# Feed-forward strips of 256 columns with a 512-column product over both halves of x, and two entry strips in turns, in a hybrid decoder trunk

## The chip, the core and the metric

The kernel runs on one core of one Trainium2 chip. The metric is the device time of one execution, in microseconds (us), median of the runs shown. The engines are named as in the profile: PE is TensorE's matmul, PEld its weight load, DVE is VectorE, ACT ScalarE, POOL GpSimd, SP the SyncE queue that issues the DMAs.

## The reference

Two decoder layers over 256 tokens of width 2048, in float32. The first has an S5 and an RWKV-7 mixer, the second a Hawk recurrent block; each layer ends with a dense SwiGLU feed-forward part of inner width 5632. Each of the four parts stands between two RMS norms with a residual. Only the feed-forward part and the norms ahead of it are touched:

```python
def swiglu(h, w_gate, w_up, w_down):
    return (jax.nn.silu(h @ w_gate) * (h @ w_up)) @ w_down

# in each layer, after the mixer:
h = rms_norm(x, norm_ffn_pre[layer])
x = x + rms_norm(swiglu(h, ffn_w_gate[layer], ffn_w_up[layer], ffn_w_down[layer]),
                 norm_ffn_post[layer])
```

## The kernel before

Activations stand transposed: features on the 128 partitions, in chunks k of 128, and the 256 tokens along the free axis. A matrix product takes a 128 x 128 block of the weight as stationary operand and a chunk of x (128 x 256) as moving operand. Float32 accuracy comes from three products in fp32r: weight and x are each split into a high and a low part, and hi by x-high, hi by x-low and lo by x-high are added up in PSUM (L513, L514, L515 in `Strip.run`). That is a block of three products, each with its own weight load.

Weights arrive in chunks of 512 KB: 128 partitions by 2 rows of k by 512 columns (`fetch`, SP's queue, the tile `raw`). `ready` splits a chunk: ACT copies it into `hi` (L136), DVE subtracts into `lo` (L112). From the middle of the program on the rings of raw, hi and lo are four deep, and `Strip.take` has a chunk's split issued some three chunks ahead of its use. A strip is 512 output columns over all of k: four output tiles in two PSUM banks (`psw`, two generations, so that the next strip uses the other pair).

A feed-forward part (`ffn`) goes in two halves of the inner width. A half has 11 strips of gate and up (256 columns of each), evacuated by `gate` (multiply by the norm's factor `rb`, Silu, multiply, split into `hhi` and `hlo`), then four strips of the down product over the half's 22 chunks of the hidden vector; the first half's sums are copied to `y` (`first_evac`), the second's are added (`last_evac`), with their squares summed for the next norm.

Between the parts stands `post`. It makes the norm's factor (`token_rstd`, `rstd_steps`), then, chunk by chunk, the residual sum `xr` (DVE and POOL), x-high `xh` (ACT) and x-low `xl` (DVE). The first strip behind it, the entry strip, runs while x is being made: before each of its eight chunk pairs `before(g)` issues the making of the next two x chunks, `behind(g)` their squares. The factor of the norm itself is only known at the end of the entry (`finish`), so the entry strip's evacuation waits for it (`late`, `lazy`). There are three entries: two into a feed-forward part, one into the Hawk block.

The order on each engine is the order in which the program issues. Small work (evacuations, norms) is put into lanes of generators and issued between the products when a planner's clock `L.now` says that its inputs are due; `L.now` goes up by a fixed amount per block.

Of the kernel before, what the change touches and what calls it, by code (L numbers as in the profile page):

```python
# [67 lines left out]
def build(tc, a, out):  # L68
# [149 lines left out]
    with ctx:  # L218
# [185 lines left out]
        def fetch(upto):  # L404
            while nraw[0] < min(upto, len(groups)):
                w, g = groups[nraw[0]]
                wp = ring(nraw[0], "raw")
                t = wp.tile([P, 2, w.shape[3]], F32, tag="raw", bufs=1 if wp is wps[1] else 3, name="raw")
                SY.dma_start(t, w[g])
                clk["D"] = max(clk["D"], splt.get(nraw[0] - RAW[0], 0.0)) + 1.46 * w.shape[3] / 512  # L410
# [4 lines left out]
        def ready(upto):  # L415
            while nhi[0] < min(upto, len(groups)):
# [4 lines left out]
                W = raw.shape[2]  # L421
                hi = wp.tile([P, 2, W], F32R, tag="hi", bufs=1 if wp is wps[1] else 3, name="hi")
                lo = wp.tile([P, 2, W], F32R, tag="lo", bufs=1 if wp is wps[1] else 3, name="lo")
# [36 lines left out]
        class Strip:  # L460
# [19 lines left out]
            def take(self, g, less=0):  # L480
# [65 lines left out]

        def strip(w, x, widths, evac, hook=None, tail=False, mid=None, lazy=False, lane="ev"):
# [6 lines left out]

        W4 = [P] * 4

        def of2(z):

            return lambda k: (z[0][k // 8][:, k % 8, :], z[1][k // 8][:, k % 8, :])

# [12 lines left out]
        w_fg = [[a["w_fg"][l, i] for i in range(22)] for l in range(2)]  # L573
        w_fd = [[[a["w_fd"][l, h, s] for s in range(4)] for h in range(2)] for l in range(2)]

        def plan_ffn(l):
            for h in range(2):
                plan(*w_fg[l][11 * h:11 * h + 11], *w_fd[l][h])
# [1001 lines left out]
        def post(y, ssq, gpost, gpre):  # L1580
# [4 lines left out]
            xs = ([slot8(name="xh0"), slot8(name="xh1")], [slot8(name="xl0"), slot8(name="xl1")])  # L1585
            sx = Ssq(1)
            keep_warm(7)
            got, at = {}, {}

            def add(k, e):  # L1590
                t, xk = tmp1(("pn", "cs", "sw", "av")[k % 4]), xr[:, k]
                stt(V, t, y[k // 8][:, k % 8], vc(gpost, k), rs, MUL, MUL)
                if k == 1:
                    low(0)
                tt(e, xk, xk, t, ADD)

            def high(k):
                act(xs[0][k // 8][:, k % 8], xr[:, k], AF.Copy, scale=vc(gpre, k))

            def low(k):  # L1600
                stt(V, xs[1][k // 8][:, k % 8], xr[:, k], vc(gpre, k),
                    xs[0][k // 8][:, k % 8].bitcast(F32), MUL, SUB)
                at[k] = clk["V"] + 0.13

            def before(g):
                if g == 0:
# [6 lines left out]
                for k in (2 * g + 2, 2 * g + 3):  # L1613
                    if k < 16:
                        high(k)
                for k in (2 * g + 2, 2 * g + 3):
                    if k < 16:
                        low(k)
                    if k < 14:
                        add(k + 2, G)  # L1620
                if g == 6:
                    rel(rs)

            def behind(g):
                sq = sx.place()
                act(sq, xr[:, 2 * g:2 * g + 2], AF.Square)
                sx.pair(sq)
                if g == 7:
# [13 lines left out]
            return of2(xs), (before, behind, at.get), got  # L1642

        def ffn(l, x, mid, rstd, fp, gain=None):
            y = None
            rb = []
            for hf in range(2):
                hh = [fp.tile([P, 22, T], F32R, tag=n, name=n) for n in ("hhi", "hlo")]
                have = set()

                def late(i):
# [5 lines left out]
                    return f  # L1657

                def gate(i):
                    def f(ps):  # L1660
# [7 lines left out]
                        def rest():  # L1668
# [3 lines left out]
                            split(hh[0][:, 2 * i:2 * i + 2], hh[1][:, 2 * i:2 * i + 2], ga)  # L1672
                            have.add(i)
# [11 lines left out]
                def need(g):  # L1685
                    if g not in have:
                        L.drain("ev")
                        assert g in have

                for s in range(4):  # L1690
                    strip(w_fd[l][hf][s], of1(hh), W4, last_evac(y, s, ssq, True, gain) if hf else first_evac(y, s),
                          need, tail=bool(hf and s == 3))
# [30 lines left out]
        with tc.tile_pool(name="f0", bufs=1) as fp:  # L1723
            y, ssq = ffn(0, x, mid, rstd, fp)
            x, mid, rstd = post(y, ssq, "n0d", "n1a")


        with tc.tile_pool(name="hk", bufs=1) as hk:
# [81 lines left out]
            for n in range(8):  # L1810
                strip(w_oi[n], x, W4, hawk(n), lane="hx", **({} if n else dict(mid=mid, lazy=True)))
# [46 lines left out]
def pack(inp):  # L1858
# [56 lines left out]
    fg, fd = [], []  # L1915
    for l in range(2):
        k = np.stack([kt(g[n][l]).reshape(8, 2, P, 22, 256) for n in ("ffn_w_gate", "ffn_w_up")], 4)
        fg.append(k.transpose(3, 0, 2, 1, 4, 5).reshape(22, 8, P, 2, 512))
        fd.append(np.stack([strips(g["ffn_w_down"][l][2816 * j:2816 * j + 2816], 512) for j in range(2)]))
    o["w_fg"] = f(np.stack(fg))  # L1920
    o["w_fd"] = f(np.stack(fd))
# [4 lines left out]
          "w_fd", "s5lam", "s5bc", "s5d", "w2a2", "g2"]  # L1926
# [17 lines left out]
```

## Time and profile before

| | us |
|---|---|
| median of 3 runs (2434.27 to 2438.75) | 2435.07 |
| the profiled execution | 2434.1 |
| its span, first to last instruction | 2432.3 |
| PE busy | 2358.0 (97%) |
| DVE busy | 1457.4 (60%) |
| ACT busy | 1180.8 (49%) |

Busy time counts an instruction from its start to its modelled end, so products that overlap in the pipeline make PE look full; the distance from one product's start to the next says more. Times in the views are us from the span's start unless marked ns. The granted clock is a share of TensorE's full 2.4 GHz.

### The profile page before, as it was taken

What the parts mean: (1) busy time and instruction counts of PE and PEld (TensorE: products, weight loads), DVE (VectorE), ACT (ScalarE), POOL (GpSimd) and SP (SyncE); (2) the same over time, 40 slices, a digit from 0 to 9 for tenths busy, and PEclk for the clock granted to TensorE, in tenths of its full rate; (3) what the DMA queues carried; (4) which work ended last, traced back from release to release, by engine and by line L of the source; (5) the groups of instructions that cost most, each with busy time, mean ns of one, the idle gap of its engine ahead of it and who ended that gap; (6) DMA issues with size and microseconds to landing.
All of it is one profiled execution on the core that took longest, in us unless ns stands there. A gap on an engine that the chain in (4) does not pass through costs nothing.

```text
span 2432.3 us, 47365 instructions
## 1 busy us (share of the span) xinstructions
PE 2358.0 (97%) x19830; PEld 2313.1 (95%) x19830; DVE 1457.4 (60%) x2002; ACT 1180.8 (49%) x1550; POOL 410.5 (17%) x589
## 2 busy tenths in 40 slices
PE   7888999998999999999999999998999999999997
PEld 7888888998999999999999899998999999999997
DVE  9786667568655544555544877757555544555544
ACT  5566545445444444444443687945444444444443
POOL 4773665515000000000000400014000000000002
PEclk8899999999999999999999999999999999999999
DMA  5222534454555555555554455564555555555553
GB/s 199 65 87 83 157 111 134 122 176 148 182 184 185 185 184 184 185 182 186 182 183 164 156 179 194 173 195 137 185 182 187 182 187 186 183 182 183 185 187 114
DMA packets 127446, 404.21 MB, mean 166 GB/s; under 512 B 26112, under 2 KB 26880, under 8 KB 127104
## 3 DMA queue, kind: packets, MB, share of 16 engines
q1 hardware_dynamic: 126912, 399.61, 50.1%
q8 instruction: 155, 2.54, 0.4%
q0 software_dynamic: 320, 1.58, 0.2%
q14 instruction: 59, 0.48, 0.1%
HBM read 397.98 MB, written 3.15 MB: 165 GB/s over the span
## 4 chain that ended last, share of the span: by engine, by line
PE 74%; DVE 3%; POOL 1%; ACT 1%; issue 1%; POOLq 0%; ACTq 0%; DVEq 0%
PE psw L513 24%; PE psw L515 24%; PE psw L514 24%; DVE lo L112 1%; DVE xl L131 1%; POOL xr L112 1%; ACT hi L136 0%; PE ssq L263 0%; PE warm L263 0%; PE own L515 0%; PE own L514 0%; PE own L513 0%; POOL sqs L112 0%; DVE sqs L112 0%; POOL tg L112 0%
## 5 line engine op out<-in xcount | busy, mean ns | idle before, releaser
L112 DVE TENSOR_TENSOR lo<-raw,hi 128x1024 fp32r<-128x1024 f32 (+1 forms) x760 | 931.6, 1230 | 868.9 <-ACT hi L136 867.2
L136 ACT ACTIVATE hi<-raw 128x1024 fp32r<-128x1024 f32 (+1 forms) x760 | 783.7, 1035 | 931.6 <-PE psw L514 733.1
L514 PE MATMUL psw<-xl,hi 128*128 128x256 f32 x3328 | 943.3, 283 | 15.1 <-DVE xl L131 14.8
L513 PE MATMUL psw<-xh,hi 128*128 128x256 f32 x3328 | 942.5, 283 | 0.9 <-ACT xh L136 0.9
L515 PE MATMUL psw<-xh,lo 128*128 128x256 f32 x3328 | 941.4, 283 | 0.0
L514 PEld LDWEIGHTS psw<-xl,hi 128*128 128x128 f32 x3328 | 635.9, 191 | 19.8 <-DVE xl L131 19.8
L513 PEld LDWEIGHTS psw<-xh,hi 128*128 128x128 f32 x3328 | 635.9, 191 | 1.5 <-ACT xh L136 1.5
L515 PEld LDWEIGHTS psw<-xh,lo 128*128 128x128 f32 x3328 | 636.2, 191 | 0.0
L515 PE MATMUL psw<-hhi,lo 128*128 128x256 f32 x1364 | 384.8, 282 | 0.0
L513 PE MATMUL psw<-hhi,hi 128*128 128x256 f32 x1364 | 384.8, 282 | 0.0
L514 PE MATMUL psw<-hlo,hi 128*128 128x256 f32 x1364 | 384.3, 282 | 0.0
L112 POOL TENSOR_TENSOR sqs<-sqs 128x512 f32<-128x512 f32 x44 | 73.0, 1659 | 1519.2 <-ACT sqs L136 1518.7
L514 PEld LDWEIGHTS psw<-hlo,hi 128*128 128x128 f32 x1364 | 257.9, 189 | 0.0
L513 PEld LDWEIGHTS psw<-hhi,hi 128*128 128x128 f32 x1364 | 257.9, 189 | 0.0
L515 PEld LDWEIGHTS psw<-hhi,lo 128*128 128x128 f32 x1364 | 257.9, 189 | 0.0
L513 PE MATMUL psw<-hh,hi 128*128 128x256 f32 x560 | 173.7, 310 | 4.8 <-ACT hi L136 3.2
L514 PE MATMUL psw<-hl,hi 128*128 128x256 f32 x560 | 164.2, 293 | 5.4 <-DVE hl L131 5.4
L515 PE MATMUL psw<-hh,lo 128*128 128x256 f32 x560 | 164.5, 294 | 4.0 <-DVE lo L112 3.9
L513 PEld LDWEIGHTS psw<-hh,hi 128*128 128x128 f32 x560 | 111.1, 198 | 12.7 <-issue 5.8
L514 PEld LDWEIGHTS psw<-hl,hi 128*128 128x128 f32 x560 | 111.6, 199 | 6.3 <-DVE hl L131 6.0
L515 PEld LDWEIGHTS psw<-hh,lo 128*128 128x128 f32 x560 | 111.3, 199 | 5.7 <-DVE lo L112 5.5
L136 ACT ACTIVATE ga<-ga 128x512 f32<-128x512 f32 x52 | 32.8, 632 | 83.0 <-DVE ga L112 82.9
(424 smaller groups left out, 2719.9 us busy)
## 6 DMA issues: line engine op xcount, KB each, us to landing
raw<-in_w_fg SPq DMA_DIRECT2D x352, 512.0 KB, 3.5
raw<-in_w_fd SPq DMA_DIRECT2D x176, 512.0 KB, 3.5
raw<-in_w_oi SPq DMA_DIRECT2D x64, 512.0 KB, 4.0
raw<-in_w_p SPq DMA_DIRECT2D x64, 384.0 KB, 3.2
raw<-in_w_eo SPq DMA_DIRECT2D x32, 512.0 KB, 3.6
raw<-in_w_oo SPq DMA_DIRECT2D x32, 512.0 KB, 3.7
raw<-in_w_u SPq DMA_DIRECT2D x16, 512.0 KB, 4.4
raw<-in_w_glu SPq DMA_DIRECT2D x8, 512.0 KB, 3.5
```

The costliest lines, as they stand in the source:

```text
L112: e.tensor_tensor(o, x, y, op=op)
L131: e.scalar_tensor_tensor(o, x, s, y, op0=op0, op1=op1)
L136: S.activation(o, x, f, bias=bias, scale=scale)
L513: TE.matmul(o, hi[:, kk, sl], xh, start=st, stop=False, skip_group_check=True)
L514: TE.matmul(o, hi[:, kk, sl], xl, start=False, stop=False, skip_group_check=True)
L515: TE.matmul(o, lo[:, kk, sl], xh, start=False, stop=en, skip_group_check=True)
```

## The change

The feed-forward strips after the entry become 256 columns wide (`PairStrip`): chunks of 4 rows of k by 256 columns, still 512 KB. x-high and x-low of one k stand side by side in SBUF, so that one product of 512 columns multiplies the hi block with both; its two halves fall into the two halves of a PSUM bank. The lo block is multiplied with x-high alone, 256 columns, into the first half. A block has two products in place of three. The evacuation adds the two halves of a bank: ACT copies one, DVE adds the other (`sums`).

Each entry into a feed-forward part now runs two 512-wide strips in turns, by a list (`TURNS`), and the making of x is spread over eleven turns (`make`). The halves of the inner width become 24 and 20 chunks. The last strip of the second half stays 512 wide. In the norm's step three chunks are split before the warming products, and the sum of squares is issued a microsecond later.

```diff
@@ rstd_steps
             if warm:
+                ready(cur[0] + 3)
                 keep_warm(warm)
@@ fetch, ready
-                t = wp.tile([P, 2, w.shape[3]], F32, tag="raw", ...)
+                t = wp.tile(list(w.shape[1:]), F32, tag="raw", ...)
...
@@ Strip.take
                 if self.mid:
                     self.mid[0](g)
+                    less = less or sum(z() for z in self.mid[3:])
                 ready(i + min(HL[0], max(2, i - 1)) - less)
@@
+        class PairStrip(Strip):
+            def run(self, g, i, hi, lo, ns):
+                stall(dep(hi, lo), "split")
+                for kk in range(4):
+                    k = 4 * g + kk
+                    x = self.x(k)
+                    for n in range(2):
+                        L.pump()
+                        sl = slice(P * n, P * n + P)
+                        o = self.ps.t[n]
...
+                        TE.matmul(o, hi[:, kk, sl], x, start=k == 0, stop=False, skip_group_check=True)
+                        TE.matmul(o[:, 0], lo[:, kk, sl], x[:, 0], start=False, stop=k == 4 * self.kg - 1,
+                                  skip_group_check=True)
+                        L.now += 0.35
+                used[i] = L.now
+
+        def strips_in_turns(a, b):
+            for z, g in TURNS:
+                (a, b)[z].go(g)
...
+        w_fg = [[a["w_fg"][l, i] for i in range(2)] + [a["w_fn"][l, i] for i in range(40)] for l in range(2)]
+        w_fd = [[[a["w_fa"][l, s] for s in range(8)], [a["w_fb"][l, s] for s in range(6)] + [a["w_fc"][l]]]
+                for l in range(2)]
+        HF = (24, 20)
+        TURNS = [(0, 0), (1, 0), (0, 1), (1, 1), (0, 2), (1, 2), (0, 3), (1, 3), (0, 4), (0, 5), (1, 4),
+                 (0, 6), (1, 5), (0, 7), (1, 6), (1, 7)]
@@ post
+            make = (0, 2, 3, 5, 7, 9, 10) if two else range(7)
...
+            def xr_at(k):
+                rdy[xr.tensor.name] = when.get(k, 0.0)
...
+            def more(j):
+                for k in (2 * j, 2 * j + 1):
+                    high(k)
+                for k in (2 * j, 2 * j + 1):
+                    low(k)
+                    if k < 14:
+                        add(k + 2, G)
...
             def before(g):
-                if g == 0:
+                if turn[0] == 0:
...
+                if turn[0] in make:
+                    more(make.index(turn[0]) + 1)
...
+            def ahead():
+                return ((turn[0] > 0) + (1 < turn[0] <= make[6])) if two else 0
 
             def finish():
                 yield from after(sx.buf)
+                yield 1.0
                 yield from sx.flush()
@@ ffn
-                hh = [fp.tile([P, 22, T], F32R, tag=n, name=n) for n in ("hhi", "hlo")]
+                hh = fp.tile([P, 24, 2, T], F32R, tag="hh", name="hh")
...
-                for i in range(11):
-                    strip(w_fg[l][11 * hf + i], x, W4, late(i) if hf == i == 0 else gate(i),
-                          **(dict(mid=mid, lazy=True) if hf == i == 0 else {}))
+                def sums(ps, o):
+                    for j in range(2):
+                        act(o[:, j], ps.t[j][:, 1], AF.Copy)
+                    for j in range(2):
+                        tt(V, o[:, j], ps.t[j][:, 0], o[:, j], ADD)
+
+                def narrow(k):
+                    def f(ps):
+                        ga = fp.tile([P, 2, T], F32, tag="ga", bufs=2, name="ga")
+                        sums(ps, ga)
+                        tt(V, ga, ga, rb[0], MUL)
+
+                        def rest():
+                            act(ga[:, 0], ga[:, 0], AF.Silu)
+                            yield from after(ga)
+                            tt(V, ga[:, 0], ga[:, 0], ga[:, 1], MUL)
+                            yield from after(ga)
+                            keep(k, 1, ga[:, 0:1])
+                        return rest()
+                    return f
+
+                if hf == 0:
+                    strips_in_turns(*[Strip(w_fg[l][i], x[0], W4, late(i), mid=mid, lazy=True) for i in range(2)])
+                for i in range(20):
+                    pair_strip(w_fg[l][2 + 20 * hf + i], x[1], narrow(i + 4 * (1 - hf)))
...
+                def down(s):
+                    def f(ps):
+                        o = y[s // 4][:, 2 * (s % 4):2 * (s % 4) + 2]
+                        if hf == 0:
+                            sums(ps, o)
+                            return None
+                        ub = fp.tile([P, 2, T], F32, tag="ub", bufs=2, name="ub")
+                        sums(ps, ub)
+                        tt(V, o, o, ub, ADD)
...
+                for s in range(6 if hf else 8):
+                    pair_strip(w_fd[l][hf][s], ofp(hh), down(s), need(4))
+                if hf:
+                    strip(w_fd[l][1][6], lambda k: (hh[:, k, 0], hh[:, k, 1]), W4,
+                          last_evac(y, 3, ssq, True, gain), need(2), tail=True)
@@ build
-            x, mid, rstd = post(y, ssq, "n0d", "n1a")
+            x, mid, rstd = post(y, ssq, "n0d", "n1a", two=False)
```

The weights are laid out for this on the host, with the same bytes in all.

## Rows read from the trace of the kernel before

**Rows 1.** The page: busy time of each engine, and the chain that ended last.

```profile
PE 2358.0 (97%) x19830; PEld 2313.1 (95%) x19830; DVE 1457.4 (60%) x2002; ACT 1180.8 (49%) x1550; POOL 410.5 (17%) x589
...
PE 74%; DVE 3%; POOL 1%; ACT 1%; issue 1%; POOLq 0%; ACTq 0%; DVEq 0%
PE psw L513 24%; PE psw L515 24%; PE psw L514 24%; DVE lo L112 1%; DVE xl L131 1%; POOL xr L112 1%; ACT hi L136 0%; PE ssq L263 0%; PE warm L263 0%; PE own L515 0%; PE own L514 0%; PE own L513 0%; POOL sqs L112 0%; DVE sqs L112 0%; POOL tg L112 0%
```

**Rows 2.** Timeline of PE in a steady strip: start, duration, instruction, count; 34 left out.

```profile
1199.81 0.28 PE L513 MATMUL psw<-xh,hi 128*128 128x256 f32 x1
...
1204.01 0.28 PE L515 MATMUL psw<-xh,lo 128*128 128x256 f32 x1
```

**Rows 3.** Stages: window, length; PE, PEld, DVE, ACT, POOL busy; clock, DMA share, GB/s.

```profile
105.00:111.00 6.00, 5.64 (x26) 5.39 (x27) 5.34 (x8) 5.90 (x10) 2.77 (x3) 0.50 0.33 94
700.00:900.00 200.00, 200.00 (x1679) 200.00 (x1678) 101.11 (x94) 82.47 (x86) 0.00 (x0) 1.00 0.56 185
1700.00:1900.00 200.00, 200.00 (x1674) 200.00 (x1674) 109.03 (x107) 83.14 (x89) 0.00 (x0) 1.00 0.55 184
```

**Rows 4.** Timeline of PE in the window of the lower clock, weights 32 and 128 wide.

```profile
106.38 0.42 PE L513 MATMUL psw<-hh,hi 128*32 128x256 f32 x1
106.60 0.41 PE L514 MATMUL psw<-hl,hi 128*32 128x256 f32 x1
...
107.24 0.41 PE L514 MATMUL psw<-hl,hi 128*128 128x256 f32 x1
107.45 0.41 PE L515 MATMUL psw<-hh,lo 128*128 128x256 f32 x1
```

**Rows 5.** Timeline of PE: products of 64 columns, two to a row; four left out.

```profile
98.73 0.39 PE L263 MATMUL py<-spr,cb 128*128 128x64 f32 x2
...
99.40 0.28 PE L263 MATMUL py<-spr,cb 128*128 128x64 f32 x1
```

**Rows 6.** Timeline of PE: three steps behind 32-wide weights, in two places; two left out.

```profile
96.29 0.28 PE L513 MATMUL psw<-hh,hi 128*32 128x256 f32 x1
...
96.64 0.28 PE L513 MATMUL psw<-hh,hi 128*128 128x256 f32 x1
...
97.35 0.28 PE L513 MATMUL psw<-hh,hi 128*32 128x256 f32 x1
...
97.69 0.28 PE L513 MATMUL psw<-hh,hi 128*128 128x256 f32 x1
```

**Rows 7.** Stages: the entries into the two feed-forward parts.

```profile
565.00:599.00 34.00, 27.55 (x214) 25.72 (x212) 32.65 (x43) 21.73 (x33) 27.71 (x21) 1.00 0.43 138
1650.00:1684.00 34.00, 28.04 (x218) 26.22 (x216) 32.63 (x40) 21.77 (x34) 28.08 (x21) 1.00 0.43 138
```

**Rows 8.** Timeline of DVE in the first entry; the idle time before, with its releaser.

```profile
561.72 0.48 DVE L131 SCALAR_TENSOR_TENSOR pn<-ya,vec,rstdp 128x256 f32<-128x256 f32 x1 [0.80 <-PE rstdp L263]
...
577.41 1.36 DVE L112 TENSOR_TENSOR lo<-raw,hi 128x1024 fp32r<-128x1024 f32 x1
578.69 0.94 DVE L131 SCALAR_TENSOR_TENSOR xl<-xr,vec,xh 128x256 fp32r<-128x256 f32 x1
...
581.38 1.37 DVE L112 TENSOR_TENSOR lo<-raw,hi 128x1024 fp32r<-128x1024 f32 x1
```

**Rows 9.** Timeline of PE in the first entry: waits for x-low and for the squares.

```profile
579.69 0.39 PE L514 MATMUL psw<-xl,hi 128*128 128x256 f32 x1 [0.84 <-DVE xl L131]
...
599.01 0.61 PE L263 MATMUL ssq<-ones,sqs 128*128 128x1 f32 x4 [0.80 <-DVE sqs L112]
```

**Rows 10.** Timelines of DVE and ACT: operations of 256 columns that read PSUM.

```profile
557.91 0.42 DVE L112 TENSOR_TENSOR yb<-own,yb 128x256 f32<-128x256 f32 x1
...
603.79 0.39 ACT L136 ACTIVATE rstd<-rstdp 128x256 f32<-128x256 f32 x1 [0.94 <-PE rstdp L263]
```

**Rows 11.** Groups, 900 to 1300 us: busy us, mean ns, idle before, what ended it.

```profile
L112 DVE TENSOR_TENSOR lo<-raw,hi 128x1024 fp32r<-128x1024 f32 x140 | 171.6, 1226 | 197.4 <-ACT hi L136 197.4
L136 ACT ACTIVATE hi<-raw 128x1024 fp32r<-128x1024 f32 x140 | 148.2, 1058 | 213.2 <-PE psw L514 176.1 <-issue 32.9 <-PE psw L515 4.2
L112 DVE TENSOR_TENSOR ga<-psw,rstd 128x512 f32<-128x512 f32 x11 | 7.6, 692 | 0.0
```

More of the change, by code (lines that the diff above doesn't have):

```diff
@@ L1577, in build, with post @@
         z.tail()
-        def post(y, ssq, gpost, gpre):
+        def post(y, ssq, gpost, gpre, two=True):
             L.drain("ev")
             rs = token_rstd(ssq)
-            xs = ([slot8(name="xh0"), slot8(name="xh1")], [slot8(name="xl0"), slot8(name="xl1")])
+            xs = [slot8(name=f"x{j}") for j in range(4)]
+            x_ = of4(xs)
             sx = Ssq(1)
             keep_warm(7)
-            got, at = {}, {}
+            make = (0, 2, 3, 5, 7, 9, 10) if two else range(7)
+            got, at, when, turn = {}, {}, {}, [0]
+            def xr_at(k):
+                rdy[xr.tensor.name] = when.get(k, 0.0)
             def add(k, e):
@@ L1612, in before @@
                     add(3, G)
[L1613 to L1622, printed above, removed]
-            def behind(g):
[L1625 to L1628, printed above, removed]
+                if turn[0] in make:
+                    more(make.index(turn[0]) + 1)
+            def behind(g):
+                t = turn[0]
+                turn[0] += 1
+                if t == 0:
+                    square(0)
+                if t in make:
+                    square(make.index(t) + 1)
+                if t == make[6]:
                     L.add("ev", finish())
+            def ahead():
+                return ((turn[0] > 0) + (1 < turn[0] <= make[6])) if two else 0
             def finish():
                 yield from after(sx.buf)
+                yield 1.0
                 yield from sx.flush()
@@ L1640, in finish @@
                 got["rstd"] = sb
-            return of2(xs), (before, behind, at.get), got
+            return (x_, of4p(xs)), (before, behind, at.get, ahead), got
         def ffn(l, x, mid, rstd, fp, gain=None):
@@ L1657, in late, with keep @@
                     return f
+                def keep(k, n, x):
+                    split(hh[:, k:k + n, 0], hh[:, k:k + n, 1], x)
+                    have.update(range(k, k + n))
                 def gate(i):
@@ L1683, in ffn, with need, f, rest @@
                     ssq = Ssq(3)
[L1685 to L1692, printed above, removed]
+                def need(kc):
+                    def f(g):
+                        if any(k not in have for k in range(kc * g, kc * g + kc)):
+                            L.drain("ev")
+                            assert all(k in have for k in range(kc * g, kc * g + kc))
+                    return f
+                def down(s):
[7 more added lines that the diff above has]
+                        tt(V, o, o, ub, ADD)
+                        def rest():
+                            sq = ssq.place()
+                            act(sq, o, AF.Square)
+                            yield from after(sq)
+                            ssq.pair(sq, G)
+                            if gain:
+                                for k in (2 * s, 2 * s + 1):
+                                    z = y[k // 8][:, k % 8]
+                                    act(z, z, AF.Copy, scale=vc(gain, k))
+                        return rest()
+                    return f
+                for s in range(6 if hf else 8):
[3 more added lines that the diff above has]
+                          last_evac(y, 3, ssq, True, gain), need(2), tail=True)
             return y, ssq
@@ L1810, in build @@
             for n in range(8):
[L1811 removed]
+                strip(w_oi[n], x[0], W4, hawk(n), lane="hx", **({} if n else dict(mid=mid, lazy=True)))
                 if n:
```

74 lines of the change are left out of this document (54 added, 20 removed).

## The prediction, made before the changed kernel was run

> **What bounds the kernel now.** I read the page's busy table first: the matmul engine (PE) is busy 97% of a span of 2432.3 us, VectorE (DVE) 60%, ScalarE (ACT) 49%, GpSimd 17% [rows 1]. The chain that ended last says the same: 74% of it is PE, nearly all on L513, L514 and L515, the three products of a weight block; DVE, at 3%, is next [rows 1]. A full PE is no PE at its peak, so the second view is the spacing of the products in a steady strip. In [rows 2] two starts stand 4.20 us apart with 35 equal steps between them: 120 ns each. Over 200 us the stage view counts 1679 products, (200 + 0.28) / 1679 = 119.3 ns, with a granted clock of 1.00 [rows 3]. A block of three therefore takes 358 ns.
>
> What are these 119.3 ns? At a granted clock of 0.50 [rows 3], which is the 1.2 GHz level, products of 256 columns follow each other by some 213 ns whether their weights are 128 or 32 wide [rows 4]: 256 / 1.2, one column a cycle and nothing else. So at 2.4 GHz, the level of 1.00, the columns take 106.7 ns, and 12.7 ns are left over. Two rows tell where they may belong. Products of 64 columns with full loads need 0.67 us for six, 112 ns each: that is what the load chain alone takes [rows 5]. Products of 256 columns with loads only 32 wide need 0.34 us for three steps in one place, 113 ns each, and 0.35 in another, 117 [rows 6]; the streaming alone thus has 6 to 10 ns over. Load and stream together cost more than either: the leftover is a price of each load-and-product turn as far as these rows go. No row shows a product of 512 columns.
>
> The third reading is of the entries, where a feed-forward part starts before its x is made. There 34 us hold 214 products (218 in the second), worth 25.5 (26.0) us at 119.3 ns: 8.5 and 8.0 us are lost [rows 7]. DVE paces them: a round of one weight split (lo, 1.36 us) and two x chunks takes 3.97 us from lo to lo [rows 8], while PE's work for it is 24 x 119.3 ns = 2.86 us, and PE waits in each round for the xl that it needs [rows 9].
>
> **The change part by part.** The terms are set against the profiled execution's own 2434.1 us (span 2432.3), 1.0 below the median of 2435.07.
>
> *Products.* Per layer the narrow strips hold 40 x 32 = 1280 blocks of gate and up, 8 x 48 = 384 of the first down half and 6 x 40 = 240 of the second: 1904, in both layers 3808. Each loses one load and one instruction; the streamed columns stay 768. A 256-wide product with its load keeps its measured 119.3 ns. The 512-wide one is not in the trace. Bounds: below, bare streaming with the load under it, 512 / 2.4 = 213.3 ns at one column a cycle [rows 4]; above, twice a present product, 238.7 ns, if the leftover goes with the columns. Between them lies the leftover as a price per turn: 213.3 + 12.7 = 226.0, or 219.6 with the 6 ns of the quiet stream [rows 6]. I take 226.0, as the row nearest in kind is the steady turn of a full load with an fp32r stream [rows 2]. The block is then 226.0 + 119.3 = 345.3 ns against 358.0, 12.7 saved, **48 us** in all. Ends: 25.4 x 3808 = 97 us and 0.
>
> The Trainium skill has a rule that speaks against this gain. The page "TensorE: Matmul & The Clock Gate", section "Back-to-back issue gap", gives N / 2.4 + 2.5 ns: 109.2 for 256 columns and 215.8 for 512. By it three products would take 327.6 and the pair 325.0, an estimate of 10 us for 3808 blocks. The measured 119.3 lies 10 ns above the rule, so the trace doesn't agree and the measurement decides; that a load already hidden can bring nothing is the second rival below.
>
> *Evacuation.* A narrow strip must add its two halves: two ACT copies and two DVE adds of 256 columns. Nearest rows: ACT 0.39 us reading 256 from PSUM, DVE 0.42 reading 256 from PSUM [rows 10]. Per narrow gate strip DVE then has four weight splits of 1.23, two adds of 0.42, one 512-wide multiply of 0.69 and two 256-wide operations of 0.42: 7.3 us. ACT has four of 1.06 and four of about 0.4: 5.8 us [rows 10, 11]. PE's strip is 32 x 0.345 = 11.0 us. DVE goes from 54% [rows 3] to some 66%, ACT from 42% to 53%. It costs nothing on the path while it lies under the next strip, which has the other pair of banks; the serial chain copy, add, multiply is about 2.3 us of those 11. Queued behind the added waits are the weight splits, four chunks deep: one chunk is 2.76 us, so a split issued three chunks ahead has about 8 us, and a 2.3 us delay fits. Without that cover, 2.3 us on each of 108 strips would be 250 us. A gain is excluded, as the work is only added. What is late next is again PE.
>
> *DMA.* Chunks keep 512 KB and 4 KB per partition; the queue is loaded about 55% in the steady stages [rows 3] and goes to some 57%. Nothing on the path.
>
> *Entry strips in turns.* Two strips share each made x, so PE has 5.7 us of work per pair of x chunks where DVE's bare making of one pair, 3.97 less the split's 1.36, is 2.6 us [rows 8]. Up to the last pair DVE has 8 x 2.6 + about 9 splits x 1.36 = 33 us (three splits are moved ahead of the broadcast of rstd by the new call in the rstd step), PE 10 turns x 2.86 = 28.6 us, and DVE starts some 2 us before PE. About 2.5 us of the loss remain in each, and 6.0 and 5.5 go: **11.5 us**, the wait for the sum of squares among them (0.80 idle before ssq in PE's queue [rows 9], which a microsecond's delay in the order should remove). The third entry (the Hawk layer) keeps its single strip; it wins the same wait, **1 us**. The early splits stand on DVE between rsqrt and the first multiply, where 0.80 us is idle [rows 8], against 1.36 of a split, so one may delay x by 0.6 and save 1.36 off the ramp later: taken as 0. Together **12.5 us**, ends -3 (the early splits late in front of the x chain, about 1 us in each of three entries) and 20 (all the waiting gone).
>
> *Order only.* The remembered times of xr, the planner's 0.35 and the new shape of the hidden tile change which instruction is issued first, not how many; the last strip of each layer stays 512 wide with three products, and so does the tail after it. 0.
>
> Sum: 2434.1 - 48.4 - 12.5 = 2373.2; with the 1.0 to the median, **2374**.
>
> **The rivals.**
> *The load hides altogether.* Under 213 ns of streaming a load chain of 112 ns [rows 5] ends long before it is needed, so the 512-wide product may pay nothing over. Block 332.6, saving 25.4: 2435.1 - 96.7 - 12.5 = 2326. For it: nothing is over at the slow clock [rows 4]. Against: 6 ns are over at 2.4 GHz where the load is small [rows 6].
>
> *The removed load was hidden, the leftover belongs to the columns.* If an fp32r stream at 2.4 GHz simply runs slower than a column a cycle, the load lies beside it for nothing and the 512-wide product doubles. By the 117 ns steps with small loads [rows 6] it is 234 and the block 353.3: saving 4.7 x 3808 = 18, time 2405; by the whole 119.3 it is 0, time 2423. The page of the Trainium skill named above, in its section "What happens when you issue a matmul", lets the next load pass while a matmul streams; at the slow clock the trace agrees, at the fast one it shows the 12.7 ns. For it: the small load still leaves most of the excess there. Against: the 113 ns steps; a fixed rate would not have them.
>
> *Slower: DVE and ACT in series.* Each new step of a narrow strip passes between the two engines, and both queues run in order. If DVE waited out every ACT step (four splits of 1.06, two copies, one Silu, one hi), its gate strip would be 7.3 + 4.2 + 1.6 = 13.1 us against PE's 11.5 before. On 80 gate strips that is 132 us; the 1248 down blocks and the entries give back 16 + 12.5: 2435 + 132 - 28, about 2539. It decides from 4.2 us of exposed waiting in a strip on. For it: DVE already stands idle for ACT before its splits, 197 us in 400 [rows 11]. Against: ACT itself is held there by the products that free its buffers, 176 us in the same stretch, so the wait is PE's pace and not ACT's.
>
> *The turns do nothing.* Then 2374 + 12.5 = 2387, inside the range.
>
> **How the numbers follow.** Forecast, with the block between 339 and 349 ns: 0.60. Load hidden (2326): 0.13. Columns, 0.19, of which 0.12 near 2405 and 0.07 near 2423. Slower: 0.05. Every gain cancelled by something not listed: 0.03. The range reaches from the hidden load, 2326, to the partial column case, 2405; 2423, 2539 and no change stay out, 0.15. About 0.2%, 5 us, is what a measurement of this kernel can tell from no change. Faster holds all of the first three cases, 0.92; same 0.03; slower 0.05.
>
> **What would show it.** In a steady narrow strip the step from the 512-wide product to the 256-wide one should be 226 ns and the next 119; 213 or 239 would prove a rival. PE should have 3808 products fewer, about 16,020. DVE should be 66% busy in gate strips with no PE wait on hi, lo or the banks. In the two feed-forward entries PE's idle time before xl should be under 3 us. The forecast is wrong if the pair's steps are not these, or if PE shows waits on psw at strip starts.

## The result and the profile after

The changed kernel takes 2397.11 us (median of 4 runs, 2394.17 to 2399.03) against 2436.91 for the kernel before (2434.27 to 2439.12): ratio 0.9841, 95% interval 0.9829 to 0.9853. That is 39.8 us less, where 61 were forecast. The direction, the range and the mechanism held; both terms of the sum were too large. The profiled execution is 2398.39 us long, its span 2396.5.

First the page of the kernel after, its busy table, the chain that ended last, and the groups of the new products (L569 is the 512-column product, L570 the 256-column one behind it, L515 to L517 are the three products where strips stayed 512 wide):

```profile
PE 2329.9 (97%) x16022; PEld 2124.1 (89%) x16022; DVE 1537.6 (64%) x2298; ACT 1257.1 (52%) x1830; POOL 410.6 (17%) x589
...
PE 74%; DVE 3%; POOL 1%; ACT 1%; issue 0%; POOLq 0%; ACTq 0%
PE psw L569 37%; PE psw L570 19%; PE psw L515 6%; PE psw L516 6%; PE psw L517 6%; DVE lo L112 1%; DVE x L131 1%; POOL xr L112 1%; PE ssq L263 0%; PE own L516 0%; PE own L517 0%; PE own L515 0%; POOL sqs L112 0%; POOL tg L112 0%; DVE sqs L112 0%
...
L569 PE MATMUL psw<-x,hi 128*128 128x512 f32 x2560 | 891.6, 392 | 0.0
L570 PE MATMUL psw<-x,lo 128*128 128x256 f32 x2560 | 718.2, 281 | 0.0
```

There are 16,022 products, 3808 fewer than in [rows 1], and PE is still the chain, with the same 74%. The idle time before both groups is 0.0: no wait on hi, lo, x or a PSUM bank in 2560 blocks. So the added evacuation and the wait for the banks are hidden.

The stages, as in [rows 3] (window, length; PE, PEld, DVE, ACT, POOL busy with their counts; clock, DMA share, GB/s):

```profile
700.00:900.00 200.00, 200.00 (x1148) 175.58 (x1147) 117.66 (x145) 96.06 (x132) 0.00 (x0) 1.00 0.58 189
1050.00:1150.00 100.00, 100.00 (x576) 87.94 (x575) 62.27 (x82) 50.27 (x72) 0.00 (x0) 1.00 0.59 189
1700.00:1900.00 200.00, 200.00 (x1151) 175.83 (x1151) 125.05 (x162) 100.08 (x145) 0.00 (x0) 1.00 0.59 190
```

574 blocks in 200.3 us make 349 ns each; three products took 358 [rows 3]. PEld, full in [rows 3], now has 12% of the time free. In the middle row, gate strips only, DVE is at 62% and ACT at 50%. DMA went from 185 to 189 GB/s, and nothing waits for it.

One strip of gate and up at close range (PE's timeline: start, duration, instruction, count):

```profile
799.81 0.40 PE L569 MATMUL psw<-x,hi 128*128 128x512 f32 x1
800.04 0.28 PE L570 MATMUL psw<-x,lo 128*128 128x256 f32 x1
800.16 0.40 PE L569 MATMUL psw<-x,hi 128*128 128x512 f32 x1
800.39 0.28 PE L570 MATMUL psw<-x,lo 128*128 128x256 f32 x1
...
890.06 0.40 PE L569 MATMUL psw<-hh,hi 128*128 128x512 f32 x1
890.29 0.28 PE L570 MATMUL psw<-hh,lo 128*128 128x256 f32 x1
```

The starts are 230 and 120 ns apart, 0.35 us a block; over whole strips the steps average 230.6 and 117.6 in gate strips and 232.0 and 119.4 in down strips (the steps between starts, averaged over all narrow blocks of the trace). The forecast's pair, 226 + 119.3, lies 3 to 6 ns below. Over all narrow strips a block takes 349.3 ns. That is midway between the forecast's 345.3 and the 353.3 of the milder column rival, so these steps alone do not decide between the two; e4 does.

Where did the time go? The products that broadcast a norm's factor (`rstdp`) mark the parts: the first feed-forward part of the kernel after is the time between these two rows, 752.88 us.

```profile
564.56 0.62 PE L263 MATMUL rstdp<-cst,rs 128*128 128x128 f32 x4
...
1317.44 0.62 PE L263 MATMUL rstdp<-cst,rs 128*128 128x128 f32 x4
```

| from rstd to rstd, us | before | after | e1: products as before |
|---|---|---|---|
| mixer of the first layer (code unchanged) | 514.9 | 519.1 | 522.6 |
| first feed-forward part, with its entry | 772.4 | 752.9 | 769.7 |
| Hawk block, with its entry | 313.1 | 311.7 | 311.7 |
| second feed-forward part, with its entry | 772.0 | 753.6 | 770.4 |

The parts that were changed lost 19.5, 1.4 and 18.4 us, 39.3 together, which accounts for the 39.8 of the medians. The profiled executions differ by only 35.7 because the mixer, whose code is the same, happened to run 4.1 us longer; over the traces of this study it takes from 514 to 523 us, so it is no effect of the change.

### The profile page after: what moved, and what is told of

The parts are those of the page before. It is cut to its first block, busy times and chain, and to the rows that moved or that the text cites. A ratio compares the mean times of both kernels' runs of the same rounds, so it can differ in the third digit from the quotient of the medians.

```text
span 2396.5 us, 40310 instructions
## 1 busy us (share of the span) xinstructions
PE 2329.9 (97%) x16022; PEld 2124.1 (89%) x16022; DVE 1537.6 (64%) x2298; ACT 1257.1 (52%) x1830; POOL 410.6 (17%) x589
## 4 chain that ended last, share of the span: by engine, by line
PE 74%; DVE 3%; POOL 1%; ACT 1%; issue 0%; POOLq 0%; ACTq 0%
PE psw L569 37%; PE psw L570 19%; PE psw L515 6%; PE psw L516 6%; PE psw L517 6%; DVE lo L112 1%; DVE x L131 1%; POOL xr L112 1%; PE ssq L263 0%; PE own L516 0%; PE own L517 0%; PE own L515 0%; POOL sqs L112 0%; POOL tg L112 0%; DVE sqs L112 0%
## 5 line engine op out<-in xcount | busy, mean ns | idle before, releaser
L569 PE MATMUL psw<-x,hi 128*128 128x512 f32 x2560 | 891.6, 392 | 0.0
L570 PE MATMUL psw<-x,lo 128*128 128x256 f32 x2560 | 718.2, 281 | 0.0
L569 PEld LDWEIGHTS psw<-x,hi 128*128 128x128 f32 x2560 | 479.4, 187 | 107.7
L570 PEld LDWEIGHTS psw<-x,lo 128*128 128x128 f32 x2560 | 483.0, 189 | 0.0
L569 PE MATMUL psw<-hh,hi 128*128 128x512 f32 x1248 | 438.9, 395 | 0.0
L570 PE MATMUL psw<-hh,lo 128*128 128x256 f32 x1248 | 352.0, 282 | 0.0
L569 PEld LDWEIGHTS psw<-hh,hi 128*128 128x128 f32 x1248 | 234.4, 188 | 55.0
L570 PEld LDWEIGHTS psw<-hh,lo 128*128 128x128 f32 x1248 | 235.0, 188 | 0.0
L516 PE MATMUL psw<-x,hi 128*128 128x256 f32 x768 | 219.6, 286 | 5.4 <-DVE x L131 4.8
L517 PE MATMUL psw<-x,lo 128*128 128x256 f32 x768 | 218.6, 285 | 2.3 <-DVE lo L112 2.3
L515 PE MATMUL psw<-x,hi 128*128 128x256 f32 x768 | 219.3, 286 | 0.0
L515 PE MATMUL psw<-hh,hi 128*128 128x256 f32 (+1 forms) x680 | 209.2, 308 | 4.9 <-ACT hi L136 3.3
L517 PE MATMUL psw<-hh,lo 128*128 128x256 f32 (+1 forms) x680 | 199.9, 294 | 4.7 <-DVE lo L112 4.6
L516 PEld LDWEIGHTS psw<-x,hi 128*128 128x128 f32 x768 | 147.8, 192 | 7.9 <-DVE x L131 7.9
L517 PEld LDWEIGHTS psw<-x,lo 128*128 128x128 f32 x768 | 147.9, 193 | 2.7 <-DVE lo L112 2.7
L515 PEld LDWEIGHTS psw<-x,hi 128*128 128x128 f32 x768 | 148.0, 193 | 0.3 <-ACT hi L136 0.2
L515 PEld LDWEIGHTS psw<-hh,hi 128*128 128x128 f32 (+1 forms) x680 | 135.6, 199 | 13.1 <-issue 5.8
L517 PEld LDWEIGHTS psw<-hh,lo 128*128 128x128 f32 (+1 forms) x680 | 135.6, 199 | 6.5 <-DVE lo L112 6.3
```

What stands on the lines that cost most here:

```text
L515: TE.matmul(o, hi[:, kk, sl], xh, start=st, stop=False, skip_group_check=True)
L516: TE.matmul(o, hi[:, kk, sl], xl, start=False, stop=False, skip_group_check=True)
L517: TE.matmul(o, lo[:, kk, sl], xh, start=False, stop=en, skip_group_check=True)
L569: TE.matmul(o, hi[:, kk, sl], x, start=k == 0, stop=False, skip_group_check=True)
L570: TE.matmul(o[:, 0], lo[:, kk, sl], x[:, 0], start=False, stop=k == 4 * self.kg - 1, skip_group_check=True)
```

## The experiments

**e1: the new strips with three products.** Everything of the change stays, the layout, the extra evacuation, the turns, but the 512-column product becomes two of 256 with the same hi.

```diff
-TE.matmul(o, hi[:, kk, sl], x, start=k == 0, stop=False, ...)
+TE.matmul(o[:, 0], hi[:, kk, sl], x[:, 0], start=k == 0, stop=False, ...)
+TE.matmul(o[:, 1], hi[:, kk, sl], x[:, 1], start=False, stop=False, ...)
```

> The changed kernel with the 512-column product of a narrow strip taken apart again into two products of 256 columns with the same hi block (hi by x-high into one half of the bank, hi by x-low into the other); strips, turns, halves and the two-step evacuation stay. It tells the products' share of the gain from the rest. If the whole products' gain is the measured step, 349.3 ns a block against 358, the time goes up by 8.7 x 3808 = 33 us over the changed kernel, to about 2430. If the gain came from elsewhere (entries, evacuation, 4 rows of k in a chunk), the time stays near 2397. By my forecast of 12.7 ns a block it would be 2397 + 48 = 2445, which the trace of the changed kernel already speaks against.

Measured: 2432.77 us (10 runs, 2428.41 to 2435.09), ratio to the kernel before 0.9988 (0.9978 to 0.9997). PE's row of the 700 to 900 stage is back at the spacing of [rows 3], while DVE and ACT keep the added work:

```profile
700.00:900.00 200.00, 200.00 (x1677) 200.00 (x1676) 115.90 (x146) 94.47 (x130) 0.00 (x0) 1.00 0.54 183
```

So the merged product is nearly the whole gain, and the added evacuation costs nothing: DVE does 15% more work there than in [rows 3], at the same PE pace. The table above splits the gain. From e1 to the kernel after the two feed-forward parts lose 16.8 us each: 33.6 us for 3808 blocks, 8.8 ns a block. From before to e1 they lose 2.7 and 1.7, and the Hawk block 1.4: **5.8 us** for the entries and whatever else changed.

**e2: no turns.** The two entry strips run one after the other, x is made as before; the rest stays.

```diff
-TURNS = [(0, 0), (1, 0), (0, 1), (1, 1), (0, 2), ...]
+TURNS = [(z, g) for z in range(2) for g in range(8)]
-def post(y, ssq, gpost, gpre, two=True):
+def post(y, ssq, gpost, gpre, two=False):
```

> The changed kernel without the turns: the two entry strips of a feed-forward part run one after the other, x is made two chunks per turn in the first of them, and the look-ahead in the entry is not cut. It tells what the turns bring. By the traces the wait for x-low should come back, 8 us in an entry against 3, and the wait for the squares in PE's order (1.9 and 3.4 us in the changed kernel, with stretches at the lower clock behind) should go back to 0 to 1 us: the net is 1 to 3 us for each of two entries, so about 2 to 6 us slower than the changed kernel. If the turns brought the 11.5 us of my forecast it would be 11 us slower; if the wait for the squares eats them all, the same.

Measured: 2401.67 us (2398.27 to 2404.55), ratio 0.9865 (0.985 to 0.9879). Its feed-forward parts take 754.7 and 753.9 us, 1.8 and 0.2 more than with the turns. (The medians lie 4.6 apart, but the two kernels did not run side by side; the parts leave the mixer's scatter out.) PE's waits in the first entry (what waited, for whom: us in all, times, longest), for the kernel before:

```profile
PE psw L514 <- DVE xl L131: 5.4, 7, 1.6
PE ssq L263 <- DVE sqs L112: 0.8, 1, 0.8
```

The same view of e2, where the wait for the squares is gone:

```profile
PE psw L516 <- DVE x L131: 5.7, 7, 1.9
```

And of the kernel after:

```profile
PE ssq L263 <- DVE sqs L112: 1.6, 1, 1.6
PE psw L517 <- DVE lo L112: 1.5, 1, 1.5
PE psw L516 <- DVE x L131: 0.2, 1, 0.2
```

The turns do what they were made for: 5.7 us of waits for x shrink to 0.2. But they bring a wait of their own. Making x now takes eleven turns, the squares come later with it, and the product that sums them (ssq) stands in PE's in-order queue before they are ready. In the second entry of the kernel after it is worse (timelines of POOL, DVE and PE, idle time and its releaser in brackets):

```profile
1664.65 1.83 POOL L112 TENSOR_TENSOR sqs<-sqs 128x512 f32<-128x512 f32 x1 [0.72 <-ACT sqs L136]
1666.51 0.42 DVE L112 TENSOR_TENSOR sqs<-sqs 128x256 f32<-128x256 f32 x1 [1.16 <-POOL sqs L112]
1666.99 0.64 PE L263 MATMUL ssq<-ones,sqs 128*128 128x1 f32 x4 [3.14 <-DVE sqs L112]
...
1668.06 0.41 PE L517 MATMUL psw<-x,lo 128*128 128x256 f32 x1
1668.28 0.41 PE L515 MATMUL psw<-x,hi 128*128 128x256 f32 x1
```

PE stands 3.14 us for the last addition of squares on DVE, which itself waits for one of 1.83 us on POOL. Behind the gap the granted clock is 0.50 (from 1668.0 to 1670.6 us), and 14 steps are of 213 ns, the spacing of the 1.2 GHz level [rows 4], before the clock is back. From 1667.49 to 1670.84 us fifteen steps take 3.35 us in place of 1.79: another 1.5 us.

**e3: the sum of squares later.** Only the planner's delay before it grows, in the two entries with turns.

```diff
 yield from after(sx.buf)
-yield 1.0
+yield 5.0 if two else 1.0
 yield from sx.flush()
```

> The changed kernel with one number changed: in the two feed-forward entries the sum of squares is issued to PE some 5 us later instead of 1. The theory that the turns' gain was handed back by the PE instruction that waits for the squares says: the wait of 1.9 and 3.4 us at the ssq product goes to under 0.5 us, the stretch at half clock behind it in the second entry goes (16 products at 213 ns, 1.5 us), and the time falls by 4 to 7 us to about 2391. The rival says that the strip behind then waits for its banks, since the first strip's evacuation needs the factor that comes out of this sum: then PE waits on psw by as much, and nothing is gained.

Measured: 2390.95 us (2387.43 to 2396.36), ratio 0.9826 (0.9805 to 0.9847). Its parts take 751.2 and 750.4 us, 5.0 less than the kernel after in the two. PE's waits in the first entry of e3, the same view, are

```profile
PE psw L517 <- DVE lo L112: 1.5, 1, 1.5
PE psw L516 <- DVE x L131: 0.2, 1, 0.2
```

and ssq is gone from them. In the second entry PE still waits 1.2 us for ssq (the expectations of the later runs say 1.5). **e8** takes 6.5 in place of 5.0:

> The changed kernel with the sum of squares issued 6.5 us later in the feed-forward entries, without unused tiles. If the places cost the time in the last two kernels, this one takes about 2390, as with 5 us, and the ssq wait of the second entry is 0.7 us in place of 1.5. If 6.5 us was too late, PE waits on psw at the first narrow strip and it is slower than 2391.

Measured: 2391.76 us (2388.04 to 2394.41), ratio 0.981 (0.9784 to 0.9835), parts of 751.0 and 749.6; the wait for ssq in the second entry is 0.5 us. From before to e8 the parts lose 21.4, 1.4 and 22.4 us; less 33.6 for the products, the entries give 11.6. The 12.5 us of the forecast were there; the kernel as changed takes half of them.

**e4: products in a quiet place.** Behind the last output, with the other engines idle, runs of products are added whose results go nowhere: fp32r with 128-wide loads (512, 384, 256, 128 columns, then 512 and 256 in turns), with 32-wide loads, and bf16. The time of the whole, 2447.3 us, contains them.

> The changed kernel with stretches of products behind its last output, when the other engines have nothing left to do: fp32r products of 512, 384, 256 and 128 columns with loads of 128, then 512 and 256 in turns, then 512 and 256 with loads only 32 wide, then bf16 products of 512 and 256. Its time is some 50 us longer and says nothing. In the strips a 512-wide product takes 231 ns to the next start and a 256-wide one 118. If other engines' traffic causes the excess over a column a cycle, the quiet steps are 213 to 219 and 107 to 113. If it is TensorE's own price for an fp32r product, they are as in the strips, 230 and 117 to 120, and the steps in between tell columns (a straight line through 0) from turns (a line with slope 0.417 ns a column). The Trainium skill's formula (TensorE: Matmul & The Clock Gate, Back-to-back issue gap) gives 215.8 and 109.2; if bf16 keeps to it and fp32r doesn't, the excess belongs to the four-byte operands.

The timeline joins equal products to one row: start, from the first start to the last end, shape, count. One step is that time less one product's own length (0.39, 0.33, 0.28, 0.22 us for 512, 384, 256, 128 columns), divided by the count less one.

```profile
2389.66 10.61 PE L2006 MATMUL quiet<-q 128*128 128x512 f32 x46
2404.76 4.52 PE L2006 MATMUL quiet<-q 128*128 128x384 f32 x25
2410.34 2.92 PE L2006 MATMUL quiet<-q 128*128 128x256 f32 x23
2414.32 2.85 PE L2006 MATMUL quiet<-q 128*128 128x128 f32 x24
2423.63 5.72 PE L2006 MATMUL quiet<-q 128*32 128x512 f32 x24
2430.81 2.43 PE L2006 MATMUL quiet<-q 128*32 128x256 f32 x20
2434.64 5.56 PE L2011 MATMUL quiet<-q 128*128 128x512 bf16 x25
2441.78 1.91 PE L2011 MATMUL quiet<-q 128*128 128x256 bf16 x16
```

By the single starts the steps are 226.7, 173.3, 120.0 and 111 ns for the first four rows. From 256 to 512 columns they grow by 0.417 ns a column, which is 1 / 2.4: one column a cycle, with **13.3 ns over for each product** of 256 columns or more, whatever its length. This is for loads of 128 columns and for one place of the operands in SBUF; e5 shows what other places do. At 128 columns the load chain decides, at the 112 ns of [rows 5]. Behind loads of 32 columns the steps are 231.7 and 113.5: 18.4 and 6.8 over, so a smaller load makes the long product slower and the short one faster. The leftover therefore isn't simply the load's, nor simply the product's; how the two divide it stays open. In bf16 the steps are 215.8 and 109.2, with 2.5 over. The Trainium skill ("TensorE: Matmul & The Clock Gate", "Back-to-back issue gap") gives N / 2.4 + 2.5 ns for the isolated gap between two products. The bf16 rows agree to a tenth, the fp32r rows behind 128-wide loads lie 10.8 ns above it, and for fp32r the measurement decides.

512 and 256 in turns, as in a narrow strip, take 230 + 116.7 = 346.7 ns, the sum of 226.7 and 120.0. That is what the gate strips with the best of their buffers need (below), with DVE, ACT and the DMA at work; so the other engines' traffic costs the products of these strips nothing.

**e5: weights and hidden vector in like places.** By averages over the trace of the kernel after, a gate block takes 351.2 ns with the fourth of the four hi / lo buffers, 348.1 with the one behind it and 346.8 with the other two; in the down strips it takes 350.3 to 353.1. By the order in which the pools hand out space, the first three pairs stand 128 bytes past a multiple of 256 in each partition, as x does; the fourth and the hidden vector `hh` stand on a multiple. Below, like places means that weights and moving operand stand the same way. e5 moves the fourth buffer and the first layer's `hh` by 128 bytes; the second layer's `hh` moves by 256, and so keeps its kind of place.

```diff
 xr = res.tile([P, 16, T], F32, name="xr")
+res.tile([P, 32], F32, name="pad")
...
 with tc.tile_pool(name="f1", bufs=1) as fp:
+    fp.tile([P, 32], F32, name="pad")
```

> The changed kernel with two unused tiles of 128 bytes a partition, one ahead of the fourth buffers of hi and lo and one ahead of the second layer's hidden tile; nothing else. The trace of the changed kernel shows the same steps again and again for the same buffer: with x as moving operand the blocks of three hi and lo buffers take 346.8 ns and those of the fourth 351.3; with the hidden tile hh all four take 350 to 353. x and the three buffers begin 128 bytes past a multiple of 256, the fourth buffer and hh on a multiple. With the two tiles the fourth buffer and the first layer's hh stand at 128 too, the second layer's hh is moved by 256 and stands on a multiple as before. If the place within 256 bytes decides: gate and up of both layers go to 346.8 in all four buffers (640 blocks x 4.5 ns = 2.9 us), the first layer's down strips go to about 347 (624 x 4 = 2.5 us), the second's stay at 350 or more; together 5 us faster than the changed kernel, 2392. If the traffic of the other engines or the half of the memory decides, the steps stay as they were, and the time at 2397.

Measured: 2413.81 us (2411.06 to 2415.77), ratio 0.9914 (0.9898 to 0.993): 16 us slower, the opposite. The steady rows of e5, first a stage:

```profile
700.00:900.00 200.00, 200.00 (x1135) 173.34 (x1134) 116.69 (x144) 94.35 (x131) 0.00 (x0) 1.00 0.55 187
```

And its timeline of PE:

```profile
799.63 0.40 PE L569 MATMUL psw<-x,hi 128*128 128x512 f32 x1
799.87 0.28 PE L570 MATMUL psw<-x,lo 128*128 128x256 f32 x1
799.99 0.40 PE L569 MATMUL psw<-x,hi 128*128 128x512 f32 x1
800.23 0.28 PE L570 MATMUL psw<-x,lo 128*128 128x256 f32 x1
800.34 0.40 PE L569 MATMUL psw<-x,hi 128*128 128x512 f32 x1
800.57 0.28 PE L570 MATMUL psw<-x,lo 128*128 128x256 f32 x1
800.69 0.40 PE L569 MATMUL psw<-x,hi 128*128 128x512 f32 x1
```

1.06 us for three blocks, 353.3 ns each, with all four buffers: the six steps of a round are 241, 120, 235, 114, 232 and 118 ns. Only the down strips of the second layer, where `hh` still stands on a multiple of 256, take 351.1. The instructions and their order on each engine are those of the kernel after; only places differ. From the kernel after to e5 the feed-forward parts grow by 8.1 and 6.3 us and the Hawk block, whose 256-wide products also read the moved buffer, by 1.5: the 16 us. In the narrow blocks it is 3.7 ns a block.

**e6** has the pad of the fourth buffer, which moves `hh` of both layers too, and e8's delay; it missed its 2382 as e5 missed its 2392. **e10** is e5 once more on another chip; **e11** and **e7** are the kernel after once more, e11 beside e10, e7 beside e8 and e9, so that the chip can't be the cause.

> The changed kernel with the sum of squares issued 6.5 us later in the two feed-forward entries (5 us left a wait of 1.5 us at the second entry's ssq product) and one unused tile of 128 bytes ahead of the fourth buffers, which also moves hh of both layers by 128. If both effects are real and add: 2391 of the later sum alone, less 1 us of the rest of the wait, less 2.9 + 5 us of the places: about 2382. If the place brings nothing, 2390; if the factor of the norm now comes too late for the first narrow strip, PE waits on psw there and the time is above 2391.

> The changed kernel itself once more, beside the next two. The two kernels with unused tiles were slower where a gain was expected: every block of a strip fell into a six-step round of 114, 232, 118, 241, 120, 235 ns (353 a block) in place of 117, 230 (346.8), also in the three buffers whose place had not moved. If the places caused that, this run shows 117, 230 in three of four chunks of the gate strips again, and about 2397. If it was the chip or the run, it shows the six-step round here too, and about 2410.

> The kernel with the tiles ahead of the fourth buffers and of the second layer's hidden tile once more, beside the changed kernel. If the places make the slow six-step round, all gate blocks take 353 ns again and the time is about 2413; if it was that chip, 347 to 348 and about 2397.

> The changed kernel on the same chip as the one before: 348 ns a gate block and about 2397 if the places decide, whatever the chip.

| | us, median | ratio to before, 95% | gate strips, ns a block |
|---|---|---|---|
| e6 | 2409.91 | 0.989 (0.9873 to 0.9908) | 353.3 |
| e10 | 2419.06 | 0.994 (0.9902 to 0.9979) | 353.3 |
| e11 (same chip as e10) | 2404.26 | 0.9883 (0.9854 to 0.9912) | 346.8 to 348.1 with three buffers, 351.2 with the fourth |
| e7 | 2399.77 | 0.9846 (0.9825 to 0.9867) | 346.8 to 348.1 with three buffers, 351.2 with the fourth |

The pattern stays with the kernel and not with the chip. What the pads changed is that nothing stands in the other place any more. Reading the steps in order, the stream of the kernel after passes to 230 / 117 within two blocks behind a chunk of the fourth buffer and keeps it for the next three chunks. That suggests: with like places there are two rounds (repeated sequences of steps), 346.8 and 353.3, and a chunk in the other place throws the stream into the short one. It can't be the only way in: e4's turns of 512 and 256, whose operands stand in like places too, take the short round from the second pair on without it.

**e9: one of the two moved.** A theory made after the fact needs a run of its own. e9 is e8 with `hh` moved by 128 bytes in both layers, while the fourth buffer stays in its other place. If the reading holds, the down strips must now look like the gate strips: three buffers at about 347, one at 351.

```diff
 with tc.tile_pool(name="f0", bufs=1) as fp:
+    fp.tile([P, 32], F32, name="pad")
...
 with tc.tile_pool(name="f1", bufs=1) as fp:
+    fp.tile([P, 32], F32, name="pad")
```

> As the one before, with one unused tile of 128 bytes ahead of the hidden tile hh in both layers, and none ahead of the fourth buffers. Reading the patterns: where weights and moving operand stand alike within 256 bytes, the blocks go in one of two rounds, 117, 230 or the six-step one; where they differ, in a third (120, 233, 120, 224, 122, 234; 351 a block); and in the changed kernel it was a chunk of the third kind after which the fast round set in. If so, the down strips, now alike in three buffers and different in the fourth, go to the fast round in three of four chunks: 351.5 to 348 on 1248 blocks, 4 us, and the time is about 2386. If the fast round is not set in by that, the down strips stay at 351 or go to 353 and the time is 2390 to 2393.

Measured: 2388.82 us (2383.81 to 2389.59), ratio 0.9799 (0.9776 to 0.9821). Products that read `hh`, in the down strips of the first layer, as a stage (columns as above). The kernel after:

```profile
880.00:970.00 90.00, 90.00 (x514) 78.69 (x513) 0.00 (x0) 0.00 (x0) 1.00 0.58 187
```

e9:

```profile
880.00:970.00 90.00, 90.00 (x519) 79.16 (x518) 0.00 (x0) 0.00 (x0) 1.00 0.57 192
```

e5:

```profile
880.00:970.00 90.00, 90.00 (x512) 78.01 (x511) 0.00 (x0) 0.00 (x0) 1.00 0.56 187
```

514, 519 and 512 products in the same 90 us: 351, 348 and 353 ns a block. By the steps, e9's down strips take 351.4 ns with the fourth buffer, 347.9 with the one behind it and 346.5 to 346.7 with the other two, as read. Against e8 each feed-forward part is 2.0 us shorter (749.0 and 747.7 us); 624 down blocks a layer times 3.2 ns are 2.0. e9 has the lowest median of the study: 11.0 us under e7, the kernel after on the same chip, and about 2% under the kernel before.

## Why the prediction was right, and where it was off

*What bounds the kernel, and the mechanism: right for the loads that the kernel has.* The 12.7 ns over the streaming were taken for a price of each turn, on the ground of [rows 2], [rows 4] and [rows 6]. e4 measures 13.3 ns for each fp32r product of 256 columns and more behind a 128-wide load, independent of the length. The rival in which the load hides altogether needs 213 ns for 512 columns; even behind small loads it is 231.7. The rival in which the leftover belongs to the columns needs 239, or 234 in its milder form, and a slope above 0.417 ns a column; in the quiet stream the slope is 0.417. One reading was wrong all the same: the 6 ns over behind small loads [rows 6] were carried over to a product of 512 columns (219.6). There e4 has 231.7, close to the milder column rival's 234, and 113.5 for 256; so the price is one for each turn behind full loads only.

*Products: 48.4 forecast, 33.6 measured.* The direction and the count are right; the step that failed is the block after, 345.3 ns. It is 349.3 over the narrow strips, and the block before is 358.0, so that about 8.8 ns are saved in place of 12.7. The forecast's own bounds for the block, 339 to 349, just miss it. What it left out is place. [rows 3] give one mean, 119.3 ns, for products in all places, and the trace of before held the difference already: averaged by buffer, its 256-wide products on x stand 120.0 ns apart with three hi / lo buffers, as in the quiet stream, and 118.4 with the fourth; those on the hidden vector stand 118.5 to 119.0 apart with three and 119.5 with the fourth. No row showed this. So in like places and the short round the three products took 360 ns and the pair takes 346.8, and the gain is the whole 13.2 ns of a turn; in gate strips with the fourth buffer it is only 355 to 351.2. By strips, a block fell from 358.7 to 348.2 in gate and up, 10.5 ns, and from 356.7 to 351.4 in the down strips, 5.3 ns: 26.9 and 6.6 us. That the places do it is shown by e9, which brings the down strips to 348.2, and by e5, which takes nearly all blocks to 353.3.

*The range: held with some luck.* e5, the same instructions with two pads of 128 bytes, takes 2413.81 us and again 2419.06 as e10, outside the stated range that ends at 2405, with the 353.3 ns of the milder column rival. Nothing in the forecast chose the places that kept the kernel inside.

*Evacuation: 0 forecast, 0 measured.* e1 has all of it without the merged product and is no slower than the kernel before. The rival with DVE and ACT in series, 2539 us, needed PE waiting on the banks; their groups show 0.0 idle. DVE's share was foreseen at 66% in gate strips and is 62%.

*DMA: 0, held.* 56% of the queue in [rows 3], 58% after.

*Entries: 12.5 forecast, 5.8 measured.* The part on x was right: the waits for it, 5.4 us in the first entry before, are 0.2 with the turns, beside one of 1.5 us for a weight split. What failed is the sentence that "a microsecond's delay in the order should remove" the wait for the sum of squares. The sum was made for x made in seven turns; in eleven the last squares come later, and a microsecond became too short: 1.6 and 3.1 us of waiting in place of 0.8, and half-clock products behind the second. With the same delay but x made in seven turns (e2) this wait is gone. The prediction itself lists who is queued behind a new wait for the evacuation, but does not look at this moved product. e8 changes only the delay, and 11.6 us are found.

*The turns do nothing: refuted in part.* By the parts they bring 2.0 us as they stand (e2 against the kernel after) and about 8 with the later sum of squares (e2's 754.7 and 753.9 against e8's 751.0 and 749.6).

Left open is why place matters: which of hi, lo and x it depends on, and why like places have two rounds. e5, e6, e9 and e10 show that it does, at 346.8, 351 and 353.3 ns; no run shows the mechanism.

## What to carry to other kernels

Price a product by its fixed part before merging or splitting: here each fp32r product paid some 13 ns over its columns, and one product of 512 in place of two of 256 was worth about 9 ns a block (13 in the best places, 4 to 5 in others), and a PE that was 97% busy still had 1.4% to give. When a piece of work is spread over more turns, whatever is issued at a planned time behind it has to move too, above all a product in PE's in-order queue. And when equal streams run at different speeds with different buffers, look at where the buffers stand, and average steps by buffer before taking one mean as the price.

## What the runs showed of the hardware

- The fixed price of a product depends on the type: 13.3 ns over one column a cycle in fp32r, 2.5 ns in bf16, in the same quiet stretch and behind 128-wide loads of the same type (e4).
- Behind 32-wide loads fp32r products take 231.7 ns at 512 columns and 113.5 at 256, against 226.7 and 120.0 behind 128-wide ones (e4).
- Products of 512 and 256 columns in turns keep the sum of their steps, 346.7 ns, but 3.3 ns of it pass from the short to the long one (230 + 116.7 for 226.7 + 120.0).
- Places of 128 bytes in SBUF change the pace of PE: the same products took 346.8, 351 or 353.3 ns a block, and 16 us in all between the kernel after and e5. Streams of 256 columns alone took 120.0 ns in like places and about 118.5 in unlike ones (kernel before).
